# Multiplying the merged stream by W_out with Strassen's seven block products, and preparing combinations of W_out early in the second half

## The chip, the cores and the metric

The kernel runs on one core of a Trainium2 chip. That core has a matrix engine (TensorE, "PE" in the profile; its weight loads are the row "PEld"), a vector engine (VectorE, "DVE"), a scalar engine (ScalarE, "ACT"), a general engine (GpSimd, "POOL") and a queue that only starts transfers (SyncE, "SP"). ACT and POOL can start transfers too. The metric is the device time of one execution in microseconds; lower is better. All engines work through queues of their own, in order, and wait for each other where one needs what another makes.

## The reference

One residual block over 2048 tokens with 1024 features. Only the end is touched by the change, but what comes before says what the operands are:

```python
h = rmsnorm(x, norm_g[l])
proj = jnp.einsum('bsd,de->bse', h, w_in[l])            # ten column groups
...
att = chunked_rel_attention(q, k, v, rel_bias[l])       # own chunk + 8 before it, 8 heads
y_att = jnp.einsum('bsc,cd->bsd', att * jax.nn.silu(z_att), w_att_out[l])
y_conv = jnp.einsum('bsc,cd->bsd', gb * vconv * jax.nn.silu(z_conv), w_conv_out[l])
m = jax.nn.sigmoid(g_att) * y_att + jax.nn.sigmoid(g_conv) * y_conv
x = x + jnp.einsum('bsd,de->bse', m, w_out[l])          # m W_out: 2048 x 1024 by 1024 x 1024
return rmsnorm(x, final_norm_g)
```

## The kernel before

**Precision.** Every matrix product is done in three passes. An operand is split into a high part, rounded by a cast on ScalarE, and a low part, the difference, made on VectorE (`split_into`, L120; `split_pair`, L125). The passes are high x high, high x low and low x high. One split of a 128 x 512 block therefore costs a cast and a subtraction, and one block of a product is a row of matmuls into one PSUM bank of 128 x 512 numbers.

**Stages.** The big input projection comes first. It works on two halves of 1024 tokens, takes the column blocks in pairs, and does each pair by Strassen's seven products in Winograd's order (`ORDER`, L36; main loop from L710). Three pairs of each half are plain in that their weight operands are built from the raw weights (`PLAIN`); the others of the second half load what the first half stored (`operand`, L375). In the second half, once these plain pairs are through (L777), the pools of `first` are closed: `xs` (four blocks of x, 128 x 4 x 512 each), `ww` and `s`. Attention's pool `ab` takes their place, and attention then runs in between the remaining products, in steps (`attention`, L140).

The last two stages are done once per half of the tokens, `hf` = 0 and 1, each with two chunks of 512 tokens:

- the *merge* (`half_c`, L800): 16 items `(i, d)`, where `d` is one of eight feature tiles, `i` = 1 the convolution branch and `i` = 0 attention. For each item the weight `wy` is loaded and split into a buffer of the pool `wr` (four buffers), and for each of the two chunks 12 matmuls are made from four pairs of `mid` tiles. VectorE evicts the bank with the gate `gl` (L820); for `i` = 0 it adds the convolution's part (L824), and the sum `m[d, c]` is split (L825). All eight items of `i` = 1 come first, then the eight of `i` = 0; the tiles that attention left in memory are loaded in the items `d` = 3 to 6 of `i` = 1 (L813). In the first half the operand W_out is loaded and split along the way, once for both halves (`out_weights`, L829).
- the *output product* (`half_d`, L849): 16 items, a block of 128 tokens and a half of the columns each. An item is 24 matmuls (eight feature tiles, three passes, L874 to L876) into one bank of `ps_d`; then VectorE adds the residual x with the factor 0.25 (L878), ScalarE squares and sums (L883), and after the second column half the inverse root is made in thirteen small VectorE steps (`rsqrt_mean`, `newton`), two scalings follow (L887), and two stores leave by SP's queue (L888). During the items 9 to 13 of the first half the next merge's first weight, gates and `mid` tiles are loaded (`next_half`, L904).

**Buffers.** `tt` has 56 slots of 128 x 512 (`slot`), `ep` ten (`e`), `gp` five for gates and the final gain, `wr` four of 128 x 1024, `op` 24 of 128 x 512 for W_out. PSUM has eight banks: three in `ps_d`, two each in `ps_s` and `ps_t` and one in `ps_m`, which attention uses.

**Order of the work.** Only the first stage has an order written by hand. Everywhere else the listing gives the priority. The framework's planner lays the instructions into the engines' queues by the times it expects, so that an instruction that is ready can be put ahead of one written earlier that is not; a buffer is taken only when its last reader is through. `defer` and `tick` put a store a number of products later in the listing.

## Time and profile before

| | |
|---|---|
| median of 3 runs | 1555.99 us (1550.83 to 1557.67) |
| span of the profiled execution | 1555.8 us (its own time beside the span is not listed) |
| TensorE busy | 1516.6 us, 97% of the span, 7396 matmuls |
| VectorE busy | 1039.7 us, 67% |
| ScalarE busy | 680.1 us, 44% |
| POOL busy | 155.0 us, 10% |
| transfers | 389.45 MB, 250 GB/s on average |

The profile is of one execution. A line such as `L874 PE MATMUL ps_d<-wo,mh ... x192 | 74.7, 389 | 0.0` says: line 874 of the kernel, engine, operation, the output and the inputs by their names in the program, how many; then the busy time together, the mean duration in ns of one, and the time for which the engine stood idle just before them, with what ended it. In the timeline each row is start, duration, engine, line, operation; `x3` means that three of the same were merged. Matmuls overlap in the pipeline, so their durations add up to more than the time they take.

### The profile page before, as it was taken

What the parts mean: (1) busy time and instruction counts of PE and PEld (TensorE: products, weight loads), DVE (VectorE), ACT (ScalarE), POOL (GpSimd) and SP (SyncE); (2) the same over time, 40 slices, a digit from 0 to 9 for tenths busy, and PEclk for the clock granted to TensorE, in tenths of its full rate; (3) what the DMA queues carried; (4) which work ended last, traced back from release to release, by engine and by line L of the source; (5) the groups of instructions that cost most, each with busy time, mean ns of one, the idle gap of its engine ahead of it and who ended that gap; (6) DMA issues with size and microseconds to landing.
All of it is one profiled execution on the core that took longest, in us unless ns stands there. A gap on an engine that the chain in (4) does not pass through costs nothing.

```text
span 1555.8 us, 21590 instructions
## 1 busy us (share of the span) xinstructions
PE 1516.6 (97%) x7396; PEld 1267.9 (81%) x7396; DVE 1039.7 (67%) x2078; ACT 680.1 (44%) x1250; POOL 155.0 (10%) x294
## 2 busy tenths in 40 slices
PE   9899999999998999999999999999999999999997
PEld 6678888888776788888888888888888888888886
DVE  7977789796668654666666767677755574445544
ACT  6353353443325343555666556666665231112111
POOL 0000000000000001223222222322220000000000
PEclk9999999999999999999999999999999999999999
DMA  5288999988987835999898776888889945365131
GB/s 209 77 285 307 339 353 327 364 310 305 319 301 262 279 122 177 329 339 341 294 290 272 228 265 228 262 261 272 263 278 322 304 162 200 102 233 193 62 109 68
DMA packets 159406, 389.45 MB, mean 250 GB/s; under 512 B 19904, under 2 KB 40384, under 8 KB 159296
## 3 DMA queue, kind: packets, MB, share of 16 engines
q1 hardware_dynamic: 129088, 302.06, 56.2%
q0 software_dynamic: 20992, 69.22, 13.6%
q10 hardware_dynamic: 9216, 16.78, 2.9%
q8 instruction: 59, 0.97, 0.3%
q14 instruction: 51, 0.42, 0.1%
HBM read 236.99 MB, written 150.99 MB: 249 GB/s over the span
## 4 chain that ended last, share of the span: by engine, by line
PE 83%; DVE 9%; ACT 2%; DMA 2%; issue 2%; POOL 0%; SPq 0%; ACTq 0%; DVEq 0%; POOLq 0%
PE ps_d L137 20%; PE ps_d L135 20%; PE ps_d L136 20%; PE ps_d L876 4%; PE ps_d L874 4%; PE ps_d L875 4%; PE ps_s L190 4%; PE po L228 4%; PE ps_t L210 3%; DVE ptl L216 1%; DVE ps_s L196 1%; DMA wc<-wc 1%; DVE xs L304 1%; ACT pr L200 1%; DMA vv<-v 0%
## 5 line engine op out<-in xcount | busy, mean ns | idle before, releaser
L200 ACT ACTIVATE pr<-ps_s,nmax 128x640 f32<-128x640 f32 (+4 forms) x128 | 93.4, 730 | 96.7 <-DVE nmax L196 96.1
L158 POOL DMA_DIRECT2D q<-q x128 | 66.7, 526 | 681.3 <-DVE wc L123 602.5
L196 DVE CUSTOM_DVE_ANT_0 ps_s<-ps_s,bs 128x640 f32<-128x640 f32 (+4 forms) x128 | 95.4, 745 | 53.8 <-PE ps_s L190 53.2
L122 ACT CAST wc<-wraw 128x512 fp32r<-128x512 f32 x120 | 73.6, 621 | 114.2 <-PE ps_d L137 94.2
L202 ACT ACTIVATE pr<-pr,rs 128x640 f32<-128x640 f32 (+4 forms) x128 | 97.8, 764 | 27.3 <-DVE rs L201 27.2
L190 PE MATMUL ps_s<-kk,q 128*128 128x320 f32 (+1 forms) x448 | 97.4, 333 | 2.9 <-ACT pr L200 2.8
L135 PE MATMUL ps_d<-mid,wy 128*128 128x512 f32 x256 | 99.6, 389 | 0.0
L136 PE MATMUL ps_d<-mid,wy 128*128 128x512 f32 x256 | 99.6, 389 | 0.0
L137 PE MATMUL ps_d<-mid,wy 128*128 128x512 f32 x256 | 99.6, 389 | 0.0
L216 DVE TENSOR_TENSOR ptl<-ps_t,pth 128x640 fp32r<-128x640 f32 (+4 forms) x128 | 94.3, 736 | 6.6 <-ACT pth L215 6.0
L215 ACT CAST pth<-ps_t 128x640 fp32r<-128x640 f32 (+4 forms) x128 | 80.0, 625 | 41.0 <-PE ps_t L210 40.0
L123 DVE TENSOR_TENSOR wc<-wraw,wc 128x512 fp32r<-128x512 f32 x120 | 82.2, 689 | 13.7 <-ACT wc L122 13.5
L210 PE MATMUL ps_t<-ident,pr 128*128 128x128 f32 x560 | 83.9, 276 | 1.1 <-DVE ptl L216 0.6
L883 ACT ACTIVATE sq<-y 128x512 f32<-128x512 f32 x32 | 20.2, 632 | 146.0 <-DVE y L878 141.3
L228 PE MATMUL po<-pth,vv 128*128 128x256 f32 x336 | 79.1, 271 | 1.8 <-DMA vv<-v 1.6
L228 PE MATMUL po<-ptl,vv 128*128 128x256 f32 x336 | 78.3, 281 | 0.2 <-DVE ptl L216 0.2
L874 PE MATMUL ps_d<-wo,mh 128*128 128x512 f32 x192 | 74.7, 389 | 0.0
L875 PE MATMUL ps_d<-wo,mh 128*128 128x512 f32 x192 | 74.7, 389 | 0.0
L876 PE MATMUL ps_d<-wo,ml 128*128 128x512 f32 x192 | 74.7, 389 | 0.0
L190 PEld LDWEIGHTS ps_s<-kk,q 128*128 128x128 f32 x448 | 67.0, 190 | 7.8 <-ACT pr L200 7.4
L878 DVE SCALAR_TENSOR_TENSOR y<-ps_d,y 128x512 f32<-128x512 f32 x32 | 22.1, 692 | 76.0 <-PE ps_d L876 75.9
L210 PEld LDWEIGHTS ps_t<-ident,pr 128*128 128x128 f32 x560 | 63.2, 140 | 11.4 <-DVE ptl L216 2.1
(370 smaller groups left out, 4183.8 us busy)
## 6 DMA issues: line engine op xcount, KB each, us to landing
wc<-wc SPq DMA_DIRECT2D x294, 512.0 KB, 4.8
wraw<-wp_in SPq DMA_DIRECT2D x54, 512.0 KB, 5.9
q<-q POOLq DMA_DIRECT2D x128, 128.0 KB, 4.9
gl<-gate SPq DMA_DIRECT2D x64, 256.0 KB, 3.2
mid<-mid SPq DMA_DIRECT2D x64, 256.0 KB, 5.2
bs<-bias POOLq DMA_DIRECT2D x32, 320.0 KB, 7.2
gate<-c ACTq DMA_DIRECT2D x34, 256.0 KB, 4.7
v<-vst SPq DMA_DIRECT2D x64, 128.0 KB, 4.7
```

What stands on the lines that cost most here:

```text
L135: nc.tensor.matmul(ps, lhsT=w[:, 0, k, :], rhs=rh[:, cs], start=(first and k == 0), stop=False)
L136: nc.tensor.matmul(ps, lhsT=w[:, 0, k, :], rhs=rl[:, cs], start=False, stop=False)
L137: nc.tensor.matmul(ps, lhsT=w[:, 1, k, :], rhs=rh[:, cs], start=False, stop=(last and k == len(rhs) - 1))
L190: nc.tensor.matmul(ps[:, i, :m], lhsT=q[s][:, g * P:(g + 1) * P], rhs=kk[:, k1 - n + i * m:k1 - n + (i + 1) * m], start=(s == 0), stop=(s ...
L196: nc.vector.tensor_tensor_reduce(out=view, in0=view, in1=bv, scale=-0.125, scalar=3.0e38, op0=ALU.add, op1=ALU.min, accum_out=nmax)
L200: nc.scalar.activation(out, view, AF.Exp, bias=nmax, scale=-1.0, accum_out=rs)
L210: nc.tensor.transpose(out=ps[:, j * P:(j + 1) * P], in_=pr[:, j * P:(j + 1) * P], identity=ident)
L216: nc.vector.tensor_sub(lo[:, js, qs], src, hi[:, js, qs].bitcast(F32))
L228: nc.tensor.matmul(ps[:, (g0 + a) * P:(g0 + b) * P], lhsT=vv[:, g0 + j, :], rhs=s[:, j, a * P:b * P], start=(i == 0 and s is pt[0]), stop= ...
L874: nc.tensor.matmul(ps, lhsT=mh[:, gs], rhs=wh, start=(k == 0), stop=False)
L875: nc.tensor.matmul(ps, lhsT=mh[:, gs], rhs=wl, start=False, stop=False)
L876: nc.tensor.matmul(ps, lhsT=ml[:, gs], rhs=wh, start=False, stop=(k == KT - 1))
```

## The change

The output product m W_out is done by Strassen's seven block products in Winograd's form. m of one half of the tokens is cut into A11, A12 (first chunk, features 0 to 511 and 512 to 1023) and A21, A22 (second chunk), W_out into B11, B12, B21, B22. With S1 = A21 + A22, S2 = S1 - A11, S3 = A11 - A21, S4 = A12 - S2 and T1 = B12 - B11, T2 = B22 - T1, T3 = B22 - B12, T4 = T2 - B21 the products are

1: A11 B11, 2: A12 B21, 6: S2 T2, 5: S1 T1, 3: S4 B22, 7: S3 T3, 4: A22 (-T4).

The output blocks are 1 + 2; 1 + 6 + 5 + 3; 1 + 6 + 7 + 4; and 1 + 6 + 5 + 7. Each product has four blocks of 128 tokens, of 12 matmuls each.

- *Four in one bank.* For each of four token blocks, products 1, 6, 5 and 3 pile up in one bank of a new pool `ps_w`. VectorE adds the running sum to one output block after each of them. Product 2 has a bank of `ps_d`; product 7 too, and in the blocks 0 and 1 product 4 piles up on it.
- *Combinations of W_out.* `wo_steps` makes the operands 7, 5, 6 and 4 of the right side in the `xs` buffers while the plain pairs of the second half run, one step per product, and stores them to memory (`wo_d`). They are loaded in each half, as are B11, B21 and B22, and split with the factor 0.25 (`load_right`, `split_right`). `out_weights` is gone.
- *The left side* is combined in `mix`, four times per merge. The order of the merge's items (`ITEMS_C`) is now by groups of four feature tiles, so that a tile and its partner four further on are complete early; attention's tiles are loaded in the first four items.
- *Splits* are put into a list, `jobs`, and taken from it a few at a time between the products (`work`).
- *Buffers.* `op` has 12 slots of double width. The right operands 6 and 4 are split into buffers of `wr`. The pools `ps_s`, `ps_t` and `ps_m` are closed after attention, and their five banks go to `ps_w`.
- *The end of a block.* The inverse roots of two blocks are made together, except for the last two. In the first half the output's stores leave by POOL's queue, in the second by SP's.

The diff, cut to its core:

```diff
-    ITEMS_C = [(i, d) for i in (1, 0) for d in range(KT)]
+    ITEMS_C = [(i, d) for dd in ((0, 4, 1, 5), (2, 6, 3, 7)) for i in (1, 0) for d in dd]
+    def wo_steps():
+        b = {}
+        for k, h in ((1, 1), (0, 1), (0, 0), (1, 0)):
+            b[k, h] = xs.tile([P, 4, CH], F32, tag="xs", name="xw")
...
+        for j in range(4):
+            load(j + 1)
+            b11, b12, b21, b22 = (b[k, h][:, j, :] for k in range(2) for h in range(2))
+            nc.vector.tensor_sub(b12, b22, b12)
+            nc.vector.tensor_add(b11, b11, b12)
+            yield
+            nc.vector.tensor_sub(b22, b22, b11)
+            nc.vector.tensor_sub(b21, b21, b11)
+            for i, t in ((7, b12), (5, b22), (6, b11), (4, b21)):
+                keep(i, j, t)
+            for _ in range(3):
+                yield
...
+        if n == NPAIR + 2 and i == 1:
+            mixed = wo_steps()
+        if n > NPAIR + 1 and not ab:
+            next(mixed, None)
...
+    pair_slot = lambda: op.tile([P, 2, CH], F32R, tag="op", name="wo")
+    wide_slot = lambda: wtile("wo").rearrange("p s k c -> p s (k c)")
...
+        def mix(j):
+            left[1, j] = left_split(j, m[j, c0])
+            left[2, j] = left_split(j, m[4 + j, c0])
+            s1 = m[j, "s1"] = slot("s1", F32)
+            nc.vector.tensor_add(s1, m[j, c1], m[4 + j, c1])
+            nc.vector.tensor_sub(m[j, c1], m[j, c0], m[j, c1])
+            nc.vector.tensor_sub(m[j, c0], s1, m[j, c0])
+            nc.vector.tensor_sub(m[4 + j, c0], m[4 + j, c0], m[j, c0])
...
+            if n_ in (7, 10, 14, 15):
+                mix((7, 10, 14, 15).index(n_))
...
+        def product(ps, i, g, onto=False):
+            gs = slice(g * P, (g + 1) * P)
+            for j in range(4):
+                (mh, ml), w = left[i, j], right[i][j]
+                for n, (lhs, rhs) in enumerate(((mh, w[:, 0]), (mh, w[:, 1]), (ml, w[:, 0]))):
+                    nc.tensor.matmul(ps, lhsT=lhs[:, gs], rhs=rhs, start=(not onto and j == n == 0), stop=(j == 3 and n == 2), skip_group_check=onto)
...
+        chain = [ps_w.tile([P, CH], F32, tag="w", name="ps_w") for g in range(4)]
+        split_left(6)
+        split_right(6, wide_slot)
+        split_left(5)
+        load_right(5, fslot)
+        for g in range(4):
+            product(chain[g], 1, g)
+            add(g, 0, 0, chain[g])
+            work(3)
...
+        split_left(4)
+        split_right(4, wide_slot)
+        at(0)
+        for g in range(4):
+            product(chain[g], 5, g, onto=True)
+            add(g, 1, 1, chain[g])
+            work(2)
...
+        for n, (i, g) in enumerate(((7, 0), (7, 1), (4, 0), (4, 1), (7, 2), (4, 2), (7, 3), (4, 3))):
+            if i == 7:
+                held[g] = dbank("ps_d")
+                product(held[g], 7, g)
+                add(g, 1, 1, held[g], True)
+                if g > 1:
+                    add(g, 1, 0, held[g])
+            else:
+                ps = held.pop(g) if g < 2 else dbank("ps_d")
+                product(ps, 4, g, onto=g < 2)
+                add(g, 1, 0, ps, True)
+                if g == 1:
+                    normed(1, (0, 1))
+                elif g > 1:
+                    normed(1, (g,))
+            work(2)
+            at(2 + n)
```

`next_half` now loads the second merge's first tiles at the positions 1 to 4 of that last group (the order of `at`), and `add` with `last` set is followed by the square on ScalarE.

More of the change, by code (lines that the diff above doesn't have):

```diff
@@ L67, in block_kernel @@
     bias_d = [dram.tile([P, WIN], F32, name=f"bias{h}") for h in range(HEADS)]
+    wo_d = [[dram.tile([P, CH], F32, name=f"wo{i}_{j}") for j in range(4)] if i > 3 else None for i in range(8)]
     def newton(v, n):
@@ L855, in load, with split_left, one, load_y @@
-        def load(b):
-            if b < 8 and b not in ys:
-                ys[b] = [e("y") for h in range(2)]
-                for h in range(2):
-                    nc.sync.dma_start(ys[b][h], xt[8 * hf + b, :, h * CH:(h + 1) * CH])
-        load(0)
+        send = nc.sync.dma_start if hf else nc.gpsimd.dma_start
+        def split_left(i):
+            def one(j):
+                left[i, j] = split_pair("left", source[i](j))
+            jobs.extend(lambda j=j: one(j) for j in range(4))
+        def load_y(k, h):
+            for g in range(4):
+                y = ys[g, k, h] = slot("y", F32)
+                nc.sync.dma_start(y, xt[8 * hf + 4 * k + g, :, h * CH:(h + 1) * CH])
@@ new lines, in product, with done @@
+        def product(ps, i, g, onto=False):
[4 more added lines that the diff above has]
+                    nc.tensor.matmul(ps, lhsT=lhs[:, gs], rhs=rhs, start=(not onto and j == n == 0), stop=(j == 3 and n == 2), skip_group_check=onto)
+        def done(i):
+            right.pop(i)
+            for j in range(4):
+                left.pop((i, j))
@@ new lines, in half_d @@
+        chain = [ps_w.tile([P, CH], F32, tag="w", name="ps_w") for g in range(4)]
[7 more added lines that the diff above has]
+            work(3)
+        done(1)
+        load_y(1, 0)
+        split_left(3)
+        split_right(5, pair_slot)
+        split_left(7)
+        for g in range(4):
+            ps = dbank("ps_d")
+            product(ps, 2, g)
+            add(g, 0, 0, ps, True)
+            work(3)
@@ new lines, in half_d @@
+        done(2)
+        load_right(3, fslot)
+        load_y(1, 1)
+        load_right(7, fslot)
+        split_right(3, pair_slot)
+        split_right(7, pair_slot)
+        for g in range(4):
+            product(chain[g], 6, g, onto=True)
+            add(g, 1, 0, chain[g])
+            work(2)
+        done(6)
+        load_right(4, fslot)
+        load_y(0, 1)
+        split_left(4)
+        split_right(4, wide_slot)
+        at(0)
+        for g in range(4):
+            product(chain[g], 5, g, onto=True)
+            add(g, 1, 1, chain[g])
+            work(2)
@@ new lines, in half_d @@
+        done(5)
+        at(1)
+        for g in range(4):
+            product(chain[g], 3, g, onto=True)
+            add(g, 0, 1, chain[g], True)
+            if g % 2:
+                normed(0, (g - 1, g))
+            work(2)
+        done(3)
+        chain.clear()
+        held = {}
+        for n, (i, g) in enumerate(((7, 0), (7, 1), (4, 0), (4, 1), (7, 2), (4, 2), (7, 3), (4, 3))):
[5 more added lines that the diff above has]
+                    add(g, 1, 0, held[g])
+            else:
+                ps = held.pop(g) if g < 2 else dbank("ps_d")
[5 more added lines that the diff above has]
+                    normed(1, (g,))
+            work(2)
+            at(2 + n)
@@ L892, in half_d @@
+        while jobs:
+            work()
+        for i in (7, 4):
+            done(i)
         while later:
             tick()
[L895 to L901 removed]
     nxt = {}
     def next_half(n):
[L905 to L910 removed]
```

168 lines of the change are left out of this document (93 added, 75 removed).

## The prediction

> **What bounds the kernel now.** I read the page first, then the busy time by stage, then the timeline at the two places where one stage hands over to the next or to the end. From the page:
>
> ```profile
> span 1555.8 us, 21590 instructions
> PE 1516.6 (97%) x7396; PEld 1267.9 (81%) x7396; DVE 1039.7 (67%) x2078; ACT 680.1 (44%) x1250; POOL 155.0 (10%) x294
> ...
> L874 PE MATMUL ps_d<-wo,mh 128*128 128x512 f32 x192 | 74.7, 389 | 0.0
> L875 PE MATMUL ps_d<-wo,mh 128*128 128x512 f32 x192 | 74.7, 389 | 0.0
> L876 PE MATMUL ps_d<-wo,ml 128*128 128x512 f32 x192 | 74.7, 389 | 0.0
> ```
>
> TensorE is the bound, and the output product (L874 to L876) never waits: idle before it is 0.0. Next the busy time by stage. The columns are busy us and instruction count of PE, weight loads, DVE, ACT and POOL, then clock, DMA share and GB/s. The first four rows are the first gated merge, the first output product, the second merge and the second output product. Then come the end, the start of the kernel, and the plain pairs that stand before attention starts.
>
> ```profile
> 1198.50:1285.50 87.00, 87.00 (x385) 72.06 (x384) 58.27 (x92) 27.06 (x46) 1.09 (x2) 1.00 0.70 235
> 1285.50:1372.50 87.00, 87.00 (x385) 72.03 (x385) 38.57 (x127) 13.23 (x34) 0.00 (x0) 1.00 0.45 149
> 1372.50:1459.50 87.00, 87.00 (x386) 72.03 (x385) 52.79 (x91) 18.79 (x32) 0.00 (x0) 1.00 0.61 201
> 1459.50:1546.50 87.00, 87.00 (x386) 72.03 (x385) 37.22 (x124) 11.76 (x32) 0.00 (x0) 1.00 0.22 73
> 1546.50:1556.00 9.50, 0.56 (x3) 0.13 (x1) 4.16 (x16) 0.72 (x2) 0.00 (x0) 0.81 0.15 56
> ...
> 8.00:95.00 87.00, 76.10 (x318) 60.21 (x319) 76.59 (x139) 48.08 (x86) 0.00 (x0) 0.94 0.41 144
> ...
> 547.20:604.30 57.10, 57.10 (x254) 47.29 (x253) 31.95 (x48) 22.81 (x37) 0.51 (x1) 1.00 0.25 89
> ```
>
> Each of the four stages has 384 matmuls in about 87 us, so one matmul costs 87.0 / 384 = **0.2266 us**; the 389 ns of one instruction overlaps with its neighbours. TensorE has no hole from 1198 to 1547 us, and VectorE is free for half of each output product. So a matmul that goes is worth its full 0.2266 us, as long as the work put in its place is in time.
>
> **What is removed.** Today a half takes 8 token blocks x 2 column halves x 8 feature tiles x 3 passes = 384 matmuls. Afterwards it takes 7 products x 4 blocks x 4 tiles x 3 passes = 336. Two halves lose 96, and 96 x 0.2266 = **-21.8 us**, the whole possible gain.
>
> **What is added on VectorE and ScalarE.** Their price per instruction in a row comes from start-to-start times. The first seven rows are from the timeline at today's handover to the second merge, the last five from the chain of waits and the timeline at the end:
>
> ```profile
> 1373.02 0.69 DVE L878 SCALAR_TENSOR_TENSOR y<-ps_d,y 128x512 f32<-128x512 f32 x1 [4.75 <-PE ps_d L876]
> 1373.80 0.63 ACT L883 ACTIVATE sq<-y 128x512 f32<-128x512 f32 x1 [4.78 <-DVE y L878]
> 1374.34 0.19 ACT L883 ACTIVATION_READ_ACCUMULATOR sq<-y 128x1 f32 x1
> 1374.43 1.65 ACT L122 CAST wy<-wraw 128x512 fp32r<-128x512 f32 x3
> 1375.90 0.16 DVE L76 TENSOR_TENSOR ra<-ry,rv 128x1 f32<-128x1 f32 x1
> 1375.98 0.68 DVE L820 SCALAR_TENSOR_TENSOR part<-gl,ps_d 128x512 f32<-128x512 f32 x1
> 1379.96 1.89 DVE L123 TENSOR_TENSOR wy<-wraw,wy 128x512 fp32r<-128x512 f32 x3
> ...
> 1546.83 0.24 PE ps_d L876
> 1547.09 0.70 DVE y L878
> ...
> 1548.63 0.16 DVE L84 TENSOR_TENSOR rv<-ssq 128x1 f32<-128x1 f32 x1 [0.85 <-ACT sq L883]
> 1550.94 0.16 DVE L78 SCALAR_TENSOR_TENSOR ry<-ra,ry 128x1 f32<-128x1 f32 x1
> 1551.14 1.42 DVE L887 SCALAR_TENSOR_TENSOR y<-y,ry,fg_sb 128x512 f32<-128x512 f32 x2
> ```
>
> Three subtractions in 1.89 us are 0.60 us apart ((1.89 - 0.69) / 2). The output scalings (L887) are 0.67 apart, three casts 0.52, and the thirteen small steps of one inverse root take 1551.14 - 1548.63 = 2.5 us.
>
> Merge, per half: 32 evictions, 16 additions, 16 weight splits, 24 instructions of the four mixes and 8 splits of the first two right operands make 96 x 0.60 = 57.6 us of DVE beside 87 us of TensorE. Output product, per half: 20 left and 20 right splits and 30 additions (70 x 0.60 = 42.0), 16 scalings (10.7) and five inverse roots (12.5) make 65.2 us beside 336 x 0.2266 = 76.1 us. ScalarE has 40 casts (20.8) and 16 squares (0.63 + 0.19 each, 13.1), 34 us. So VectorE goes from 43% to 86% of the output product and still does not bound it on average. The cost lies in places where its work comes in a lump. I take them in order of time.
>
> (1) **The middle.** Combining W_out is 16 subtractions and additions (9.6 us), with 16 loads and 16 stores of 256 KB (8.4 MB). They are put among the plain pairs, where DVE is busy 31.95 of 57.10 us and the transfers move 89 GB/s; 8.4 MB more makes about 236. Cover is ample, so 0; if it were gone it would cost 9.6 us. Attention's buffers lie where these blocks lie. Its first load waits today for a weight split:
>
> ```profile
> 603.79 2.20 POOL L158 DMA_DIRECT2D q<-q x4 [602.49 <-DVE wc L123]
> ```
>
> Afterwards it may wait for the last stores, issued one product (2.7 us) before the end of the stretch. At some 4 us to land (loads of W_out take 4.2, stores of the output 2.1, in the DMA rows below) it starts up to 2.5 us later. TensorE has plain products to fill this with. Value 0, bounds 0 to 2.5.
>
> (2) **Start of each merge.** The 16 loads of attention's results move from items 3 to 6 to items 0 to 3, and are wanted at item 4. SP's queue then carries, per item, one weight, two gates and four of these, 1.8 MB in 5.44 us, or 337 GB/s. The loads of W_out itself (16 in the first merge) shrink to 8 per merge. Today's items 3 to 6 of the second merge show about that rate already:
>
> ```profile
> 1388.80:1410.60 21.80, 21.80 (x98) 18.06 (x97) 8.14 (x12) 2.50 (x4) 0.00 (x0) 1.00 1.01 352
> ```
>
> The transfers are full there and TensorE still has no hole. But two items then lay between the last load and its use, now one. Value 0.5 for both merges together, bounds 0 to 8 (two late loads of about 4 us).
>
> (3) **Start of each output product.** Its first product needs the fourth tile's split, written after the last item. It hangs on the item before the last, so it can run early; as written, it follows two instructions of 0.60. Value 0.3 in all, bounds 0 to 1.
>
> (4) **Fourth block on the seventh's bank.** Product 4 of a block piles up in the bank of product 7, one product (2.72 us) after the DVE has to have read it. Queued before that read are 2.5 us of inverse root and two scalings (1.3) for the blocks before. Done in that order the read ends 1 to 2.5 us late, and TensorE waits; drawn forward, as row 1375.98 shows an eviction drawn into the middle of an inverse root (L76 at 1375.90), it is in time. Behind the waiting matmul stands the rest of the output product. Value 0.5 per half, 1.0 in all, bounds 0 to 5.
>
> (5) **Handover from the first output product to the second merge.** The `wr` pool has four buffers. Right operand 4 fills all four until the very last products, and the next merge's weights need them. Today these splits run far ahead; for the second merge the last one is 15 us before its item starts:
>
> ```profile
> L135 PE MATMUL ps_d<-mid,wy x256: 389/389/389, 1198.7 to 1459.2; 128*128 128x512 f32 x128
> L123 DVE TENSOR_TENSOR wy<-wraw,wy x31: 684/691/693, 1200.1 to 1439.4; 128x512 fp32r<-128x512 f32 x31
> ```
>
> (the last item's 24 matmuls begin 5.4 us before 1459.6). Afterwards the first buffer comes free 9 matmuls, 2.0 us, before the end. A cast (0.62) and a subtraction (0.69) follow, which alone would just do. But VectorE is late by then. From the end of product 4 of block 1, TensorE has four products, 10.9 us. VectorE has six additions (3.6), two inverse roots (5.0) and six scalings (4.0), 12.6 us, and waits about 0.9 for a square. So it is 1.7 to 2.6 us behind when TensorE ends, one addition (0.6) more goes first, and the low part that the third matmul wants comes 2 to 3 us late. Behind the waiting matmul stands the whole second merge. Upper bound: the cast stands behind the last square on ScalarE and the subtraction behind the last inverse root (2.5), some 8 us. Lower bound 0. Value **2.5**.
>
> The Trainium skill, page "TensorE: Matmul & The Clock Gate", Part 1, says that an idle window of about 3.4 us halves the clock until a busy one has passed. The trace agrees as far as it goes: 0.81 granted in the 9.5 us of the end, 0.94 in the row 8 to 95 us where TensorE idles 11 us. By that rule the gap of 2.5 us costs nothing more; one of 8 us would add about 1.7, an estimate from that page.
>
> (6) **The end.** From the last matmul to the end of the span are 8.7 us today (1547.07 to 1555.8), with VectorE waiting for TensorE. In the second output product the same backlog stands before the last addition: 1.7 to 2.6 us, and up to 4 if a late start of block 0 and 1 is carried on. Value **+2.7**, bounds 0.5 to 4.5.
>
> The additions to `y`, the splits of the other operands and their loads I cost at nothing: they run one or two products (11 to 22 us) ahead of use, in a queue that is 86% full. If that cover were gone, each product would wait for four splits, 2.4 us, ten times. Stores of the first half leave by POOL's queue instead of SP's; from the DMA issues, with the time from issue to landing last:
>
> ```profile
> q<-q POOLq DMA_DIRECT2D x128, 128.0 KB, 4.9
> ...
> wraw<-wo SPq DMA_DIRECT2D x16, 256.0 KB, 4.2
> ...
> out<-y SPq DMA_DIRECT2D x32, 256.0 KB, 2.1
> ```
>
> Even 5 us to land delays only buffers that the next merge fills, and nothing on SP waits behind them.
>
> **Sum** against the profiled 1555.8: -21.8 + 0 + 0.5 + 0.3 + 1.0 + 2.5 + 2.7 = -14.8, so **1541.0 us**. The median of the runs shown is 1555.99, practically the profiled execution.
>
> **The rivals.**
>
> *Every lump is filled* (chance 0.13). The order is drawn forward everywhere, as in rows 1375.98 and 1439.4; what is left is 2 us at the end: 1536. Against it: a weight split cannot be drawn forward while its buffers are taken, as in (5).
>
> *Transfers are late at the start of the merges* (0.08). Attention's results come 4 us late twice, while the other terms stand: 1541 + 7.5 = 1548.5. For it: share 1.01 at 352 GB/s; against it: no hole in that same row.
>
> *VectorE's order as written decides* (0.07), on the slower side. If the order on VectorE keeps to the listing, the mix after items 7, 10, 14 (six instructions, 3.6 us) stands with the eviction and its addition before the next item's weight split (cast and subtraction, 1.2). TensorE then waits 5 to 6 us each time, 33 us in two halves; with 5 us twice at (4) and 8 at (5), 51 us are lost, and 1555.8 - 21.8 + 51 + 2.7 = 1588. It decides from the point where the holes exceed 21.8 us, that is from four of the six mixes. Against it: today's listing has two evictions before each split too, and no item shows a hole. For it: VectorE's idle share, which hid any wrong place in its queue, halves.
>
> The Trainium skill, page "TensorE: Matmul & The Clock Gate", table at the head, gives VectorE and ScalarE a strictly first-in first-out queue. Here three weight casts start only behind the last square (1374.34, 1374.43), which agrees.
>
> *The change is not what it says* (0.04): products 6, 5 and 3 wait for the reads of their own bank. Three other blocks (8 us) lie between; even at 0.5 us for each of 24 it is 12 us, 1553.
>
> The forecast itself has 0.68, with its own range of 1536 to 1548.
>
> **Numbers.** A measurement of this kernel tells about 0.5%, 7.8 us, from no change, so faster ends at 1548.2. Faster: nearly all of the forecast (0.66), all filled (0.13), half of the late transfers (0.04), 0.83 with rounding. Same: the rest of these and the bank waits, 0.10. Slower, over 1563.8: the listing's order, 0.07. The range holds the forecast, the filled case and most of the late transfers: 1534 to 1550.
>
> **What would show it.** 672 matmuls of 0.227 us in the output products, none other changed. Right: a hole of 2 to 3 us before the second merge's first matmuls, ended by a VectorE subtraction of `wy`; the last eviction starting 2 to 3 us after the last matmul. Wrong, if holes stand before the merge's items after a mix (order), before item 4 with a DMA as releaser (transfers), or before products 6, 5 and 3 with `y` as releaser (banks); or if attention's start pushes the merge's start past 1198.7 us.

## The result and the profile after

The kernel with the change takes 1535.43 us (1534.24 to 1537.43), beside 1555.57 for the kernel before: a ratio of 0.9878, interval 0.9857 to 0.9898, or 20.1 us less. The forecast was 1541.0 with a range of 1534 to 1550, so the sign and the range held; the sum was 5.6 us too high. The profiled execution took 1537.43 us, with a span of 1535.7.

From the page of the kernel after: the span, the busy times, and the two groups of matmuls that fill the last two stages (busy us, mean ns of one, idle just before).

```profile
span 1535.7 us, 21757 instructions
PE 1493.8 (97%) x7300; PEld 1247.1 (81%) x7300; DVE 1108.6 (72%) x2140; ACT 714.5 (47%) x1314; POOL 164.0 (11%) x310
...
L135 PE MATMUL ps_d<-mid,wy 128*128 128x512 f32 x256 | 99.6, 389 | 0.0
...
L953 PE MATMUL ps_w<-wo,lefth 128*128 128x512 f32 x224 | 69.9, 393 | 0.0
```

TensorE has 96 matmuls fewer and still no idle time before the matmuls of the two groups shown, one of an output product (L953) and one of the merges (L135); the rows below show it busy for the whole of each of the four stages. But one matmul of the output product now lasts 393 ns in the pipeline, where all of them lasted 389 before.

The busy time by stage of the kernel after, columns as in the prediction: first merge, first output product, second merge, second output product, the end; and then the first four items of each merge.

```profile
1195.80:1282.80 87.00, 87.00 (x385) 72.07 (x384) 58.26 (x91) 19.19 (x33) 1.09 (x2) 1.00 0.59 194
1282.80:1360.60 77.80, 77.80 (x337) 63.07 (x336) 62.59 (x132) 33.50 (x71) 6.50 (x12) 1.00 0.74 254
1360.60:1447.70 87.10, 87.10 (x386) 72.13 (x385) 62.11 (x116) 18.93 (x33) 2.17 (x4) 1.00 0.64 213
1447.70:1525.60 77.90, 77.90 (x337) 62.91 (x335) 62.52 (x135) 33.20 (x70) 0.00 (x0) 1.00 0.41 147
1525.60:1535.60 10.00, 0.10 (x1) 0.00 (x0) 6.17 (x24) 0.72 (x2) 0.00 (x0) 0.73 0.28 105
...
1195.80:1217.60 21.80, 21.80 (x98) 18.06 (x97) 12.28 (x19) 6.82 (x12) 1.09 (x2) 1.00 0.92 321
1360.60:1382.40 21.80, 21.80 (x98) 18.05 (x97) 13.57 (x39) 3.52 (x7) 2.17 (x4) 1.00 0.79 287
```

Where the 20.2 us between the two spans lie, from the start of one stage's first matmul to the start of the next stage's, and for the second output product to the end of its last matmul:

| | before | after | difference |
|---|---|---|---|
| start of the first merge | 1198.73 | 1195.79 | -2.9 |
| first output product | 87.04 | 77.83 | -9.2 |
| second output product | 87.20 | 77.99 | -9.2 |
| the two merges | 87.04 each | 87.04 each | 0 |
| last matmul to the end of the span | 8.77 | 9.96 | +1.2 |

So the gain is 18.4 us in the two products, less 1.2 at the end. The 2.9 us ahead of the merges are luck, not the change. Matched matmul by matmul, the kernel after is 6.3 us ahead at 530 us, and 5.3 of these arose from 400 us on, almost all before the first transfer that the change adds there (528.2 us), in code that is the same in both kernels. The profile of the kernel before has there a hole with 1.95 us of idle time, which a transfer ends (521.3 us), a stretch of half the granted clock behind it, and another such stretch from 415.7 us; the profile of the kernel after has none of the three. The hole at 565 us, shown below, then takes back 2.3 us, and the time up to the merges, mostly attention, 1.1.

The timeline of the kernel after at the handover to the second merge (TensorE starts the first matmul of the merge at 1360.66, without a gap):

```profile
1358.80 0.62 ACT L122 CAST wy<-wraw 128x512 fp32r<-128x512 f32 x1
1359.45 0.69 DVE L123 TENSOR_TENSOR wy<-wraw,wy 128x512 fp32r<-128x512 f32 x1
1360.06 0.15 DVE L86 TENSOR_SCALAR rv<-rv 128x1 f32<-128x1 f32 x1
1360.89 0.68 DVE L962 TENSOR_TENSOR y<-y,ps_d 128x512 f32<-128x512 f32 x1
...
1525.79 0.68 DVE L962 TENSOR_TENSOR y<-y,ps_d 128x512 f32<-128x512 f32 x1
1527.15 1.41 DVE L974 SCALAR_TENSOR_TENSOR y<-y,ry,fg_sb 128x512 f32<-128x512 f32 x2
1528.49 0.15 DVE L85 TENSOR_TENSOR rv<-acc 128x1 f32<-128x1 f32 x1
1530.98 1.42 DVE L974 SCALAR_TENSOR_TENSOR y<-y,ry,fg_sb 128x512 f32<-128x512 f32 x2
```

The cast of the next merge's weight runs 1.9 us before the merge starts, and the subtraction (L123) goes into the middle of an inverse root (L86 is one of its steps) that was written before it. The last four rows are the end. The last addition starts 0.1 us after the last matmul; the 1.2 us are lost afterwards, because two scalings of the block before (1527.15) stand ahead of the last inverse root. That starts 2.7 us after the last addition, where, in the kernel before, it started 1.5 us after the last eviction (1548.63 - 1547.09).

The timeline of the kernel after in the middle, where the combinations of W_out are made:

```profile
551.39 3.40 SPq L561 DMA_DIRECT2D wo<-xw  x4
554.84 2.79 SPq L558 DMA_DIRECT2D xw<-wo  x4
562.25 0.69 DVE L570 TENSOR_TENSOR xw<-xw 128x512 f32<-128x512 f32 x1 [4.62 <-DMA xw<-wo]
564.30 0.68 DVE L784 TENSOR_TENSOR u<-u,ps_d 128x512 f32<-128x512 f32 x1
565.13 0.47 PE L135 MATMUL ps_d<-t40h,wc 128*128 128x512 f32 x1 [1.98 <-DVE u L784]
```

VectorE waits 4.62 us for a load of W_out, whose issue stands behind four stores of earlier combinations in SP's queue (L561), and the evictions of the plain products (L784) stand behind that wait. TensorE then runs out of banks and has a hole of 2.4 us, up to 565.1. Holes are given here, where nothing else is said, from the start of the matmul before to the start of the one after, 2.37 us for this one; in an unbroken stream that is 0.23.

### The profile page after: what moved, and what is told of

It reads as the page before. It is cut to its first block, busy times and chain, and to the rows that moved or that the text cites. A ratio compares the mean times of both kernels' runs of the same rounds, so it can differ in the third digit from the quotient of the medians.

```text
span 1535.7 us, 21757 instructions
## 1 busy us (share of the span) xinstructions
PE 1493.8 (97%) x7300; PEld 1247.1 (81%) x7300; DVE 1108.6 (72%) x2140; ACT 714.5 (47%) x1314; POOL 164.0 (11%) x310
## 4 chain that ended last, share of the span: by engine, by line
PE 79%; DVE 10%; DMA 5%; issue 3%; ACT 3%; POOL 0%; SPq 0%; ACTq 0%; DVEq 0%; POOLq 0%
PE ps_d L137 19%; PE ps_d L135 19%; PE ps_d L136 19%; PE ps_w L953 6%; PE ps_d L953 4%; PE po L228 4%; PE ps_s L190 3%; PE ps_t L210 3%; DMA wc<-wc 1%; DMA vv<-v 1%; DVE ptl L216 1%; DMA xw<-wo 1%; DVE ps_s L196 1%; DVE xs L304 1%; ACT pr L200 1%
## 5 line engine op out<-in xcount | busy, mean ns | idle before, releaser
L135 PE MATMUL ps_d<-mid,wy 128*128 128x512 f32 x256 | 99.6, 389 | 0.0
L123 DVE TENSOR_TENSOR wc<-wraw,wc 128x512 fp32r<-128x512 f32 x120 | 81.8, 686 | 10.1 <-ACT wc L122 9.9
L953 PE MATMUL ps_w<-wo,lefth 128*128 128x512 f32 x224 | 69.9, 393 | 0.0
L228 PEld LDWEIGHTS po<-pth,vv 128*128 128x128 f32 x336 | 63.8, 190 | 6.0 <-issue 2.6
L228 PEld LDWEIGHTS po<-ptl,vv 128*128 128x128 f32 x336 | 63.8, 190 | 2.4 <-DVE ptl L216 0.2
L137 PEld LDWEIGHTS ps_d<-mid,wy 128*128 128x128 f32 x256 | 48.1, 188 | 10.1
L136 PEld LDWEIGHTS ps_d<-mid,wy 128*128 128x128 f32 x256 | 48.1, 188 | 10.0
```

What stands on the lines that cost most here:

```text
L123: nc.vector.tensor_sub(w[:, 1], src, w[:, 0].bitcast(F32))
L135: nc.tensor.matmul(ps, lhsT=w[:, 0, k, :], rhs=rh[:, cs], start=(first and k == 0), stop=False)
L136: nc.tensor.matmul(ps, lhsT=w[:, 0, k, :], rhs=rl[:, cs], start=False, stop=False)
L137: nc.tensor.matmul(ps, lhsT=w[:, 1, k, :], rhs=rh[:, cs], start=False, stop=(last and k == len(rhs) - 1))
L228: nc.tensor.matmul(ps[:, (g0 + a) * P:(g0 + b) * P], lhsT=vv[:, g0 + j, :], rhs=s[:, j, a * P:b * P], start=(i == 0 and s is pt[0]), stop= ...
L953: nc.tensor.matmul(ps, lhsT=lhs[:, gs], rhs=rhs, start=(not onto and j == n == 0), stop=(j == 3 and n == 2), skip_group_check=onto)
```

## Experiments

Three questions were open: why the matmuls of the output product got slower (231.6 ns from start to start, against 226.7 before), what the hole at 565 us needs to go away, and why none of the lumps of the forecast cost anything.

### The pace of the matmuls

Two explanations stood against each other. By the first (A), addresses do it: the change removed the little tile `ssq` (three buffers of 32 bytes), so every buffer on the left side of the memory, with the weights of these matmuls among them, lies 96 bytes lower, while `op`, the right operands on the other side, stayed. By the second (B), the busier VectorE slows TensorE.

**e1_left_shift.** An unused tile of 32 bytes moves the left side up.

```diff
+    shift = const.tile([P, 8], F32, name="shift")
+    nc.vector.memset(shift, 0.0)
```

> The changed kernel with a 32-byte tile more among the constants, which moves all buffers of the left side (tt, wr, ep, gp) up by 32 bytes and leaves op, on the right, where it is. Theory A (alignment): in the changed kernel the right operands in op start 32 bytes off a multiple of 64 and the weights in tt on one; the products that read both take 0.232 us a matmul, those with both in left-side pools (6, 4) 0.227. With both off by 32, as before the change, every product goes back to 0.2267: each output product takes 76.2 us in place of 77.8, the median falls by 3.3 us to about 1532. Theory B (VectorE and ScalarE, busier now, get in the way of TensorE's reads): nothing changes, 77.8 us and about 1535.4.

Measured: 1535.06 us, ratio 0.9882 (0.9854 to 0.9909). The two output products in the busy time by stage of this kernel:

```profile
1281.00:1357.80 76.80, 76.80 (x337) 63.05 (x336) 62.47 (x132) 33.31 (x71) 6.50 (x12) 1.00 0.75 257
1444.90:1521.90 77.00, 77.00 (x337) 62.89 (x335) 62.56 (x135) 33.25 (x70) 0.00 (x0) 1.00 0.42 149
```

One us less in each, 228.7 ns a matmul, with VectorE as busy as in the kernel after (62.5). Some six tenths of the loss are gone: addresses matter, but 32 bytes is not all of it.

**e2_before_shift.** The kernel *before*, with two constants put into one tile, so that its left side lies 32 bytes lower.

```diff
-    cw_sb = const.tile([P, 4, 3], F32, name="cw_sb")
-    cb_sb = const.tile([P, 4], F32, name="cb_sb")
+    taps = const.tile([P, 16], F32, name="taps")
+    cw_sb = taps[:, :12].rearrange("p (b w) -> p b w", w=3)
+    cb_sb = taps[:, 12:]
```

> The kernel before, with two constants in one tile, which moves the left side down by 32 bytes: tt on multiples of 64, op off by 32, as in the changed kernel, with VectorE as idle as before. Theory A (alignment): the 576 matmuls whose right operand lies in op take about 0.232 us, the 192 with it in tt stay at 0.2267; the two output products together take about 3 us more, 1558.6. Theory B (VectorE gets in the way): nothing changes, 87.0 us each, 1555.6.

Measured: 1560.64 us against 1554.96, ratio 1.0038 (1.0019 to 1.0057): slower, by 0.4%. Its two output products, by stage:

```profile
1278.20:1367.50 89.30, 89.30 (x386) 72.02 (x385) 38.58 (x126) 13.20 (x34) 0.00 (x0) 1.00 0.43 145
1454.60:1544.00 89.40, 89.40 (x385) 71.82 (x383) 37.31 (x124) 11.48 (x31) 0.00 (x0) 1.00 0.22 71
```

87.0 us became 89.3, with VectorE as idle as in the kernel before (38.6). So B falls, and a shift of one operand alone makes the old kernel slow too.

**e8_left_shift_96.** The left side moved up by the full 96 bytes.

```diff
+    shift = const.tile([P, 24], F32, name="shift")
+    nc.vector.memset(shift, 0.0)
```

> The changed kernel with a 96-byte tile among the constants, which puts the left side's buffers where the removed 96 bytes of the `ssq` tiles had them. Theory A in its second form: what counts is the distance of the right operand's address from the weights', modulo 128. It was 0 before the change (226.7 ns a matmul), 96 in the changed kernel (232 to 234), 64 with the 32-byte shift (228.8), 32 in the shifted kernel before (233.4). At 96 bytes the distance is 0 for op and for wr: 226.7 ns everywhere, 76.2 us for each output product in place of 77.8 and 76.8. Rival: the remaining 2 ns of the 32-byte shift come from the new order of reads or from a busier VectorE; then 76.8 us stay.

Measured: 1535.0 us, ratio 0.9885 (0.9865 to 0.9906). By stage:

```profile
1282.40:1358.50 76.10, 76.10 (x337) 63.04 (x336) 62.19 (x131) 33.42 (x71) 6.47 (x12) 1.00 0.75 259
1445.60:1521.90 76.30, 76.30 (x337) 62.86 (x335) 62.29 (x135) 33.32 (x70) 0.00 (x0) 1.00 0.42 150
```

**e5_op_shift_96.** The same tile put under `op` on the right side instead; the left side stays low.

```diff
     op = pool("op", 12, side="right")
+    right_shift = pool("right_shift", side="right").tile([P, 24], F32, name="right_shift")
+    nc.vector.memset(right_shift, 0.0)
```

> The changed kernel with a 96-byte tile under op on the right side: op moves down by 96 bytes, the left side stays. Distance 0 modulo 128 again, at other addresses. By the distance theory the pace is 226.7 ns and each output product takes 76.2 us; if it were the left side's own address, 77.8 us would stay.

Measured: 1535.37 us in a single run, and the first output product:

```profile
1284.00:1360.10 76.10, 76.10 (x337) 63.05 (x336) 62.16 (x131) 33.47 (x71) 6.48 (x12) 1.00 0.76 259
```

Both ways give back the old pace, so it is the distance between the two operands and not the place of either. Start addresses modulo 128 as the compiled programs have them, and the time from start to start as a mean over the whole output product:

| kernel | `op` | weights in `tt` | distance | ns per matmul |
|---|---|---|---|---|
| before | 96 | 96 | 0 | 226.7 |
| after with 96 bytes on the left (e8) | 96 | 96 | 0 | 226.7 |
| after with 96 bytes on the right (e5) | 0 | 0 | 0 | 226.7 |
| after with 32 bytes on the left (e1) | 96 | 32 | 64 | 228.7 |
| after | 96 | 0 | 96 | 231.6 |
| before, 32 bytes lower (e2) | 96 | 64 | 32 | 232.5 |

The means of the kernel after, e1 and e2 are mixed, since some of their matmuls have both operands in one pool or in two at distance 0. Inside the kernel after the same holds by product: products 3 and 5, all of whose right operands lie in `op` and weights in `tt`, take 233.3 and 233.6 ns, while product 6, whose right operand lies in `wr` at distance 0 from its weights, takes 227.5, and 226.7 from its second block on. In e1, product 3 takes 228.9; in e2, the matmuls with the right operand in `op` take 233.4. What in the chip makes the distance count was not tried.

In the whole time it doesn't show: e8 gains 3.3 us in its products, but its ratio lies inside the interval of the kernel after. The stages before the merges differ by that much between executions.

### The hole in the middle

**e3_early_loads.** All sixteen loads of W_out are issued at the first step, so that none is late.

```diff
-        load(0)
+        for j in range(4):
+            load(j)
...
-            load(j + 1)
```

> The changed kernel with all 16 loads of W_out for the combinations started at once, 4 products before the first combination, in place of four at a time. Theory C: the hole of 2.4 us on TensorE at 565 us comes from a combination on VectorE that waits for its load with evictions queued behind it; with the loads early VectorE waits for none of them after the first, the hole goes, and the median falls by about 2.4 us to 1533. Rival: the loads were held up by other transfers, so that 16 at once only move the wait to another place: a hole of 2 us elsewhere between 520 and 605 us, 1535.

Measured: 1538.17 us, ratio 0.9883 (0.9858 to 0.9908). The hole at 565 is gone but for 0.65 us. That alone does not show that the late load was its cause: VectorE no longer waits for W_out there, but 4.66 us for raw weights instead (L390, at 566.53), and the hole's size varies between profiles whose middle is the same. Over those profiles, though, it grows on the whole with VectorE's wait for the load: a wait of 2.8 us leaves a hole of 0.6 (e6), 3.5 leave 1.6 and 1.7 (e5, e8), 4.0 leave 2.1 (e11), 4.6 leave 2.4 (the kernel after), and 4.3 leave 3.2 (e7); in e1 the wait comes in two parts, 2.8 and 1.6, and the hole is 1.5. The total gained nothing that can be told: the profiled execution has a hole of 4.2 us at 731.8 in attention, ended by a load of `v`. A hole at this place, of 0.8 to 4.2 us, is in every profile here: 1.2 in the kernel after, 1.6 in e11, whose kernel is the same. So its size varies by itself, and what sets it is open.

**e4_both.** The edits of e1 and e3 together.

```diff
+    shift = const.tile([P, 8], F32, name="shift")
...
+        for j in range(4):
+            load(j)
```

> The changed kernel with both edits, the 32-byte tile and the early loads. If A and C hold, they add up: about 5.7 us below the changed kernel, 1529.7, or 0.983 to 0.984 of the kernel before. If only one of them holds, 1532 or 1533; if none, 1535.4.

Measured: 1536.1 us, ratio 0.9886 (0.9862 to 0.991); the output products take 76.84 and 77.00 as in e1. The gains did not add up. The timeline of this kernel shows a new hole in the place of the old one:

```profile
539.58 13.15 SPq L560 DMA_DIRECT2D xw<-wo  x11
552.84 7.41 SPq L563 DMA_DIRECT2D wo<-xw  x9
...
569.20 0.69 DVE L392 TENSOR_TENSOR s<-wraw 128x512 f32<-128x512 f32 x1 [5.19 <-DMA wraw<-wp_in]
```

Eleven loads of W_out and nine stores hold SP's queue for some 20 us, and the raw weights that stand behind them are late instead: VectorE waits 5.19 us, and TensorE has a hole of 2.7. In e3 nearly the same wait, 4.66 us, left a hole of only 0.65.

**e9_pool_queue.** The kernel after, with the loads and stores of the combinations issued by POOL. If SP's queue was what ran short (C2), they no longer hold anything up.

```diff
-                    nc.sync.dma_start(t[:, j, :], wo[4 * k + j, :, h * CH:(h + 1) * CH])
+                    nc.gpsimd.dma_start(t[:, j, :], wo[4 * k + j, :, h * CH:(h + 1) * CH])
...
-            defer(1, lambda: store(wo_d[i][j], t))
+            defer(1, lambda: nc.gpsimd.dma_start(wo_d[i][j], t))
```

> The changed kernel with the loads of W_out for the combinations, and the stores of the results, started by POOL's queue, idle until attention, in place of SP's. Theory C2: SP's queue is what is short there, with 16 loads, 16 stores and the raw weights of the plain pairs in one line, so that VectorE's combination or a weight split waits for its load and TensorE for the evictions behind it. With SP free of them the hole of 2.4 us at 565 us goes and none comes in its place (under 0.7 us in all between 520 and 605 us). Rival: the transfers themselves are slow, 8.4 MB beside the rest; then a hole of 1 to 2.5 us stays.

Measured: 1544.01 us, ratio 0.994 (0.9921 to 0.9959), slower than the kernel after. Two stretches of e9, from 500 and from 550 us, and the first of them in the kernel after:

```profile
500.00:550.00 50.00, 42.96 (x170) 33.80 (x171) 38.25 (x64) 13.72 (x24) 17.29 (x32) 0.93 0.98 374
550.00:605.00 55.00, 55.00 (x244) 45.37 (x243) 31.49 (x48) 22.59 (x37) 0.00 (x0) 1.00 0.34 126
...
500.00:550.00 50.00, 48.47 (x205) 39.64 (x206) 36.97 (x61) 17.09 (x29) 0.00 (x0) 0.97 0.95 330
```

From 550 us on TensorE has no hole at all, but it stands still for 7 of the 50 us before, beside 1.5 in the kernel after. There the DMA engines are busy 0.98 of the time at 374 GB/s (0.95 at 330 in the kernel after): free of SP's order, the loads start at 509.7 to 537.5 us in place of 528.2 to 557.2, and between 500 and 560 us TensorE waits 6.0 us for `wc` and VectorE 4.5 for `wraw`. So C2 falls. SP's queue was the brake that kept part of these loads out of the crowded stretch.

**e10_best.** e8 and e9 together.

```diff
+    shift = const.tile([P, 24], F32, name="shift")
...
+                    nc.gpsimd.dma_start(t[:, j, :], wo[4 * k + j, :, h * CH:(h + 1) * CH])
```

> The changed kernel with the 96-byte tile and the combinations' transfers on POOL's queue. If both theories hold: output products 76.2 us each, no hole at 565 us, 3.3 + 2.4 = 5.7 us below the changed kernel, a ratio to the kernel before of about 0.984 in place of 0.988. If only the alignment holds, 0.986.

Measured: 1542.25 us, ratio 0.9932 (0.9915 to 0.9949), with TensorE busy 42.42 of the 50 us from 500 and the products at 76.16 and 76.32. It has the loss of e9 and the pace of e8; not the best. Beside e8 on the same chip, 1535.0, from which it differs in the queue alone, the queue costs 7.2 us.

**e12_shift_gpsimd**, beside **e11_after_again**, which is the kernel after without an edit on the same chip. e12 leaves the transfers on SP and moves the sixteen subtractions and additions to POOL, with the 96 bytes of e8: the late load is then waited for on an engine that has nothing queued behind it.

```diff
+    shift = const.tile([P, 24], F32, name="shift")
...
-            nc.vector.tensor_sub(b12, b22, b12)
-            nc.vector.tensor_add(b11, b11, b12)
+            nc.gpsimd.tensor_sub(b12, b22, b12)
+            nc.gpsimd.tensor_add(b11, b11, b12)
...
-            nc.vector.tensor_sub(b22, b22, b11)
-            nc.vector.tensor_sub(b21, b21, b11)
+            nc.gpsimd.tensor_sub(b22, b22, b11)
+            nc.gpsimd.tensor_sub(b21, b21, b11)
```

> The changed kernel again, unchanged, beside the next one on the same chip. Ratio to the kernel before 0.986 to 0.990 as in its first measurement, output products 77.8 and 78.0 us, a hole at 565 us of 1 to 2.5 us.

> The changed kernel with the 96-byte tile, and the 16 subtractions and additions on W_out done by GpSimd, idle there, in place of VectorE; loads and stores stay on SP's queue. Theory C3: the hole at 565 us is VectorE's strict order, a combination that waits for its load ahead of evictions whose banks TensorE needs. With the waiting instruction on another engine the hole goes although the loads are as late as before: no hole over 0.7 us between 525 and 605 us, output products 76.2 us, 3.3 + 1.5 to 2.4 us below the changed kernel, that is a ratio to it of 0.996 to 0.997. Rival: the late transfer itself holds TensorE up, through the raw weights behind it in SP's queue; then the hole stays or moves, and only 3.3 us are gained (0.998).

Measured: 1539.17 us (1537.51 to 1544.19) for e11 and 1533.18 us (1528.60 to 1534.69) for e12; against the kernel before 0.9911 (0.9888 to 0.9934) and 0.9861 (0.9835 to 0.9887). The ranges of their times do not overlap, and the medians lie 6.0 us apart. e11 is a little slower against the kernel before than was expected (0.986 to 0.990). e12 by stage and in the timeline:

```profile
550.00:605.00 55.00, 55.00 (x244) 45.34 (x243) 31.16 (x45) 19.38 (x32) 19.07 (x21) 1.00 0.55 196
1280.50:1356.60 76.10, 76.10 (x337) 63.04 (x336) 62.19 (x131) 33.54 (x71) 6.47 (x12) 1.00 0.74 259
...
560.71 0.69 DVE L789 TENSOR_TENSOR v<-u,ps_d 128x512 f32<-128x512 f32 x1 [1.14 <-PE ps_d L139]
560.87 1.30 POOL L572 TENSOR_TENSOR xw<-xw 128x512 f32<-128x512 f32 x1 [1.85 <-DMA xw<-wo]
```

POOL waits 1.85 us for the load while VectorE goes on evicting, and TensorE is busy for all of the 55 us, where the seven profiles with the combinations on VectorE and the loads in fours on SP's queue have holes of 0.6 to 3.2. So C3 holds, as far as one profile can show it. The two mended terms, 3.3 us of pace and the hole (2.0 us lost in e11), are 5.3 of the 6.0; the rest is less than executions differ by. This version beats the kernel before, and the kernel after on the same chip; against the first measurement of the kernel after (0.9878) the intervals overlap, so the size of the second gain is uncertain. The move to POOL was not run without the 96 bytes.

### Why the lumps cost nothing

By theory P the planner's order hides them: it puts additions and splits that are ready into the inverse roots written before them. The rival was that VectorE simply has room for them.

**e7_listing_order.** VectorE keeps the order of the listing in both output products; the rest is the kernel after.

```diff
-    half_d(0, half_c(0, mids, made), next_half)
-    half_d(1, half_c(1, nxt["mids"], nxt["made"]), lambda n: None)
+    m0 = half_c(0, mids, made)
+    with tc.manual_schedule(engines={mybir.EngineType.DVE}):
+        half_d(0, m0, next_half)
+    m1 = half_c(1, nxt["mids"], nxt["made"])
+    with tc.manual_schedule(engines={mybir.EngineType.DVE}):
+        half_d(1, m1, lambda n: None)
```

> The changed kernel with VectorE's instructions of both output products kept in the order of the listing. The forecast's reason for 7 us of holes was lumps of VectorE work at products 4 of block 0, at the handover and at the end; the result shows none but 1.2 us at the end. Theory P: the lumps are there and the planner's order, which draws additions and the next weight split into the inverse roots and ahead of the scalings, is what fills them. In listing order TensorE waits at product 4 of block 0 (up to 5 us), and at the handover the second merge's weight splits stand behind everything of the first output product (8 to 13 us): in all 12 to 25 us more, 1547 to 1560. Rival N: the lumps were over-counted and the order hardly matters: under 3 us more, 1535 to 1538.

Measured: 1556.68 us in a single run, as slow as the kernel before (1554.4 on that chip) and inside the 1547 to 1560 that P expected. e7 by stage, from the first output product to the end, and its timeline at the handover:

```profile
1285.40:1367.20 81.80, 78.52 (x338) 62.86 (x337) 60.92 (x127) 32.91 (x69) 6.47 (x12) 1.00 0.65 225
1367.20:1460.40 93.20, 89.23 (x386) 73.09 (x385) 64.93 (x122) 20.18 (x35) 2.16 (x4) 0.98 0.66 212
1460.40:1541.30 80.90, 78.50 (x338) 62.79 (x336) 60.67 (x127) 32.39 (x68) 0.00 (x0) 1.00 0.40 144
1541.30:1554.90 13.60, 0.02 (x1) 0.00 (x0) 8.53 (x32) 1.45 (x4) 0.00 (x0) 0.63 0.21 77
...
1369.65 1.42 DVE L974 SCALAR_TENSOR_TENSOR y<-y,ry,fg_sb 128x512 f32<-128x512 f32 x2
1370.98 1.28 DVE L962 TENSOR_TENSOR y<-y,ps_d 128x512 f32<-128x512 f32 x2
1372.32 0.50 PE L135 MATMUL ps_d<-mid,wy 128*128 128x512 f32 x1 [2.17 <-DVE y L962]
...
1377.17 0.50 PE L135 MATMUL ps_d<-mid,wy 128*128 128x512 f32 x1 [1.80 <-ACT wy L122]
```

The same instructions in the written order cost 4.0, 6.1, 3.0 and 3.6 us more in the four stages than in the kernel after, 16.7 together, and the holes are in the stages where the forecast had put them: in the output product, early in the second merge, at the end. Their places are not quite the forecast's. In the output products they stand before product 4 of blocks 1 and 3 (and once before product 5), not of block 0. In the merge the additions at 1370.98 wait behind an inverse root and two scalings, and the first matmul of the second chunk waits for their bank; the second hole waits for a cast, not for the subtraction. Some 1.7 of the merge's 6.1 us come from 3.4 us at half the granted clock behind the second hole. So P holds.

**e6_more_vector_work.** One more addition after each of the thirty of a half, its result unused: 18 us more for VectorE in each output product.

```diff
+            nc.vector.tensor_add(e("extra"), y, y)
```

> The changed kernel with one more VectorE addition of 128 x 512, its result unused, behind each of the 30 additions of an output product: 30 x 0.60 = 18 us more per half, 83 us of VectorE work beside 77.8 us of TensorE. If VectorE was really 84% full, it now sets the time: each output product lasts at least 83 us, 5 us more, or up to 8 with the lumps, and the run 10 to 18 us longer, 1546 to 1553. If there is far more room than the sum says, under 3 us.

Measured: 1547.88 us in a single run. e6 by stage: first output product, second merge, end.

```profile
1288.20:1366.10 77.90, 77.90 (x338) 63.18 (x337) 74.19 (x160) 33.61 (x71) 4.47 (x9) 1.00 0.71 240
1366.10:1455.30 89.20, 87.57 (x385) 71.81 (x384) 64.98 (x119) 19.16 (x33) 4.15 (x8) 1.00 0.65 218
1533.30:1546.10 12.80, 0.06 (x1) 0.00 (x0) 9.06 (x29) 0.72 (x2) 0.00 (x0) 0.69 0.41 155
```

The time lies in the expected range, but the expectation missed. With VectorE busy 74.2 of 77.9 us TensorE still has no hole in the output product; 2.2 us spill into the merge and 2.8 into the end, 5.0 where 10 to 18 were expected. The rest of the time above the kernel after lies before the first merge, where nothing was changed (its start is 1201.2 us, against 1195.8). So room alone does not decide: 12 us more of busy time in the planner's order cost less than no more work in the written one.

## Why the prediction was right, and where it was wrong

| step | forecast | measured |
|---|---|---|
| 96 matmuls removed | -21.8 | -18.4 |
| (1) the middle | 0 | +2.3 |
| (2) start of each merge | +0.5 | 0 |
| (3) start of each output product | +0.3 | 0 |
| (4) product 4 on the bank of product 7 | +1.0 | 0 |
| (5) handover to the second merge | +2.5 | 0 |
| (6) the end | +2.7 | +1.2 |
| not in the change: the rest before the merges | 0 | -5.2 |
| sum | -14.8 | -20.1 |

The forecast of 1541.0 was counted down from a span, and times are some 1.8 us longer than spans (1537.43 beside 1535.7); beside the span of the kernel after the sum is 5.3 us too high. Of the terms, the holes (2) to (6) were 5.8 us too dear, the price of a matmul and the middle together 5.7 too cheap. That the two nearly cancel is luck, and so are the 5.2 us of the earlier stages, which carry the time to the low end of the range.

- **Removed work: count right, price wrong.** 672 matmuls stayed in the output products, as forecast. The step "a matmul that goes is worth its full 0.2266 us" took the price of those that stay as fixed. They cost 0.2316, and 672 x 0.005 = 3.3 us were lost. The predicted 0.227 us per matmul came back in e8 and e5.
- **(1) failed.** "Cover is ample, so 0" was argued from busy shares, VectorE at 31.95 of 57.10 us. The stretch was partly the wrong one: the loads start at 528.2 us and the combinations at 536.7, before the 547.2 of the row that was read, and from 500 to 550 us the transfers of the kernel after are busy for 0.95 of the time. The hole came from a wait: VectorE stood 4.62 us at L570 for a load, idle by every average, with the evictions behind it. The prediction quoted the table at the head of the Trainium skill's page "TensorE: Matmul & The Clock Gate", that VectorE's queue is strictly first in, first out, and used it only against the merges; the row at 562.25 agrees with it here, and the prediction's rule for waits, to name what stands behind them, was not applied to this one. The bound of 2.5 us that it gave was for another reason, attention's first load; that this one holds 2.3 is chance.
- **(2) right in direction.** 0.92 of the transfers' time and 321 GB/s in the first four items, near the 337 worked out, and no hole. The 0.5 was too careful.
- **(3) and (4) were nothing.** TensorE is busy for 77.80 of the 77.80 us of the first output product, and for 77.90 of 77.90 of the second. In (4) the way "drawn forward" was the one that happened; the 0.5 per half was set between it and the written order.
- **(5) is the term that failed in size.** The buffer does come free some 2 us before the end (cast at 1358.80, the merge starts at 1360.66). What failed is "So it is 1.7 to 2.6 us behind when TensorE ends, one addition (0.6) more goes first": it worked VectorE's list off in written order, though the prediction had itself shown row 1375.98, an eviction drawn into an inverse root. The thirteen small steps of an inverse root are thirteen places at which the planner can put something more urgent. e7 took that away, and the merge lost 6.1 us, inside the bounds of 0 to 8.
- **(6) half right.** The end got longer, by 1.2 us where 2.7 was forecast, within 0.5 to 4.5. The sign to look for was wrong: the last addition is not late (0.1 us), the last inverse root is.
- **The rivals.** *Every lump is filled* named 1536 with a chance of 0.13, and its mechanism is what the kernel after shows: its place for every lump was right. That its time is right too is luck, since 3.3 us of slower matmuls and the hole in the middle were made up by earlier stages. *VectorE's order as written* was not what the kernel does, but its price for the output products, the handover and the end (10 + 8 + 2.7 = 20.7 us) is near what e7 lost against no lumps (16.7 + 1.2 = 17.9). The 33 us that it put into the merges were not tried. *Transfers late at the merges* fell by the rows of (2), and *bank waits* by the 0.0 of L953 and the busy rows.
- **VectorE's load** was forecast at 65.2 us per output product and 57.6 per merge, ScalarE's at 34; the rows have 62.6 and 62.5, 58.3 and 62.1, and 33.5.

## What to carry to other kernels

Price a backlog on an engine by the order the planner will give it: a chain of small dependent steps is no block, and what is ready and urgent slips in between; measure that order's worth by fixing it once. A cheap operation that waits for a late transfer is costed by what is queued behind it, and it belongs on an engine with nothing behind it (VectorE to POOL here, part of 6.0 us). After a change of buffers compare the time per matmul before and after, not only the counts: a few bytes less in one pool cost 2% of two stages.

## What the runs showed of the hardware

- **Distance of operands.** Matmuls of 128 x 512 take 226.7 ns from start to start when right operand and weights start at the same address modulo 128 bytes, 228.9 at a distance of 64 (product 3 of e1), and 233.3 to 233.6 at 96 and 233.4 at 32 (products 3 and 5 of the kernel after; e2). Moving either operand by 96 bytes gave the 226.7 back (e8, e5). Nothing in the profile names this; only the mean (389 against 393 ns) gives it away.
- **Half pace after short holes.** After a hole with 1.95 us of idle time, in the kernel before, the next matmuls start 0.43 us apart and then return to 0.23. From its timeline:

```profile
521.34 0.59 PE L135 MATMUL ps_d<-t10h,wc 128*128 128x512 f32 x1 [1.95 <-DMA wc<-wc]
522.16 0.63 PE L137 MATMUL ps_d<-t10h,wc 128*128 128x512 f32 x1
522.59 0.63 PE L135 MATMUL ps_d<-t11h,wc 128*128 128x512 f32 x1
...
525.06 0.39 PE L135 MATMUL ps_d<-t13h,wc 128*128 128x512 f32 x1
```

  Some eight matmuls lose 0.2 us each, 1.6 us, nearly as much as the hole; the granted clock is 0.51 from 521.5 to 524.9 us. The size of the hole does not settle it. A hole with 1.95 us of idle time at 415.1 us in the same profile is followed by half pace; the same hole in the kernel after, at 414.1 and again 1.95 us, is not, and neither is the one of 1.98 us at 565.13. The Trainium skill, page "TensorE: Matmul & The Clock Gate", Part 1, puts the idle window at about 3.4 us and calls it free-running. The stretch of half pace agrees, some 3.4 us long; that a hole of 2 us can be enough, and only at times, differs from that rule as the prediction read it, by which a gap of 2.5 us costs nothing more, and the measurement decides.
- **Crowded transfers.** At 374 GB/s and a busy share of 0.98 (e9; 330 and 0.95 in the kernel after), 8.4 MB of loads and stores that start earlier cost TensorE more than they save: 1542.25 us beside 1535.0 (e10, e8).
